# An opening group of six products, one k-tile per load, in a decoder layer kernel

## The chip, the cores and the metric

One core of a Trainium2 chip. The metric is the device time of one execution in microseconds (us); smaller is better. Engines by the names of the profile: PE = TensorE (PEld its weight loads), DVE = VectorE, ACT = ScalarE, POOL = GpSimd, SP = SyncE, which issues most loads.

## The reference

One decoder layer for 256 prompt tokens and 8 sample tokens (264 columns together), width 2048, all in float32:

```python
h = rmsnorm(x, g_pre_mix); z = h @ w_in          # one projection, split by columns into
q_m, k_m, v_m, o_m, ig, fg, q_a, k_a, v_a, gate_a, gate_b = split(z)
A = mlstm(q_m, k_m, v_m, ig, fg) * sigmoid(o_m)  # 4 heads, matrix memory
B = sliding_window_attention(rope(q_a), rope(k_a), v_a)   # 32 query heads, 4 kv heads of 64, sinks
mix = (sigmoid(gate_a) * (A @ w_branch_a) + sigmoid(gate_b) * (B @ w_branch_b)) @ w_out
x = x + rmsnorm(mix); x = x + rmsnorm(conv_ffn(rmsnorm(x)))
```

## The kernel before, in words

Everything is kept transposed: features on the 128 partitions, the 264 tokens along the row. A matrix product is made tile by tile, 128 output features at a time, over 16 k-tiles of 128. To keep float32 accuracy with the fast matmul type, each operand is split into a high and a low part, and a k-tile costs three matmuls (wh x xh, wh x xl, wl x xh; L111 to L113). `product` (L86) loads up to 8 weight tiles of 128x128 at once into `raw` (SP's queue), ScalarE casts them to `wh` (L102), VectorE subtracts to `wl` (L103), TensorE accumulates in one PSUM bank per product (`acc`, four of them). Weight buffers come in threes, so casts run at most two loads ahead of TensorE. `one` is a product of a single output tile: two loads of 8 k-tiles. `group` (L119) makes n products together, k-tile by k-tile; before, only the first six up-projections of the feed-forward part use it, with `up_chunk` (L909).

The opening: 18 warming matmuls (L155); then the four tiles of attention keys and values are made as one product of four (L192) whose k-cuts are 1, 1, 2, 2, ... tiles. For each cut `load_x` (L179) loads the inputs `xr`, scales them by the norm's weight into `xh` (ScalarE, L186) and `xl` (VectorE, L187); squares for the norm are added up in `xacc`. The norm's factor `rstd` comes from `xacc` by small matmuls (`rs`, L160), a square root, a Newton step and a transposing broadcast (`rb`, L229, L231), and is copied to `rstd` (L235). It isn't needed in the product, only behind it: the rotary tables in `katt` are multiplied by it (L245, L246). `rope` (L248) turns a tile: a shuffle and a multiplication on VectorE, a multiplication and an addition on GpSimd (`sh` L252, `qr` or `kro` L253). Turned keys are split into `KZh`, `KZl`, values are transposed (`vt`) and split into `VHL`.

Then 16 query tiles follow, four per group g of heads: `one`, `rope`, a cast of the turned tile to `Qh` on ScalarE (L449), the low part `Ql` (L450) and the sample columns `qbd` (L452) on GpSimd.

The order of work beside the products is written out by hand: `launch` queues a generator, and `step` (L68), called after each `one`-load (half a product), starts a waiting generator when the step clock allows and moves every running one on to its next `yield`. `half` (L291) is the attention of half a head group: score matmuls (`s`, L301 and L303), row maxima, exponentials, and some steps later transposes of the probabilities (`pt`) and their product with the values. The halves are launched 7 steps apart, the first right behind the fourth query product. Within this, a scheduler lays out each engine's instructions in the order in which its own model of time sees them become ready, earlier-written ones first, and those in a `high_priority` block ahead; each engine then runs its list strictly in order. `paced` adds an order between two instructions of one engine and no wait.

## Time and profile before

| | us |
|---|---|
| median of 3 runs (lowest, highest) | 1776.38 (1773.03, 1777.71) |
| profiled execution: time; span of its instructions | 1774.99; 1773.2 |
| busy: PE / PEld / DVE / ACT / POOL | 1745.8 / 1728.8 / 1222.5 / 831.0 / 259.3 |
| mean granted TensorE clock | 0.995 |

An engine's busy time is the time in which one of its instructions runs. A row of a timeline gives the start, the duration, engine, line, operation, the tile written and the tiles read, and in brackets the idle time of the engine before it and whose work ended that. Matmuls are pipelined: the start of one to the start of the next is its cost, and the durations overlap. Releasers are worked out from semaphores.

### The profile page before, as it was taken

How to read it: one execution, taken by the hardware profiler on the slowest of the kernel's cores; microseconds unless marked ns; L12 is line 12 of the kernel's file. 1: busy time of each engine (PE TensorE's matmuls, PEld its weight loads, DVE VectorE, ACT ScalarE, POOL GpSimd, SP SyncE). 2: the span in 40 equal slices, each digit the busy share in tenths (PEclk: the TensorE clock that was granted, in tenths of full speed). 3: DMA queues.
4: the chain of work that ended last, by engine and by line, in shares of the span. 5: the costliest groups of instructions: out<-in, count | busy, mean ns of one | idle time of the engine just before them, and what ended most of it. 6: DMA issues, size and time to landing. Idle time of an engine off the chain costs nothing.

```text
span 1773.2 us, 34988 instructions
## 1 busy us (share of the span) xinstructions
PE 1745.8 (98%) x14146; PEld 1728.8 (97%) x14146; DVE 1222.5 (69%) x2278; ACT 831.0 (47%) x1166; POOL 259.3 (15%) x446
## 2 busy tenths in 40 slices
PE   9999999999999999999999999999999999999996
PEld 8999999999999999999999899999999999999996
DVE  7788867546788798756644798777777777444444
ACT  6556555334555555444444554444444444434442
POOL 2542010000111121100022430000000001000002
PEclk9999999999999999999999999999999999999998
DMA  7444475555889888865555455555555555656663
GB/s 252 160 143 144 155 228 184 220 180 189 273 273 314 304 303 290 289 211 180 179 181 173 143 173 187 182 181 184 187 179 185 183 180 184 181 182 184 182 182 119
DMA packets 104090, 354.81 MB, mean 200 GB/s; under 512 B 11690, under 2 KB 16698, under 8 KB 103928
## 3 DMA queue, kind: packets, MB, share of 16 engines
q1 hardware_dynamic: 89176, 300.06, 50.9%
q0 software_dynamic: 14752, 52.52, 8.8%
q8 instruction: 110, 1.80, 0.4%
q14 instruction: 52, 0.43, 0.1%
HBM read 328.21 MB, written 24.32 MB: 199 GB/s over the span
## 4 chain that ended last, share of the span: by engine, by line
PE 83%; DVE 5%; DMA 5%; ACT 2%; issue 2%; POOL 2%; POOLq 0%; SPq 0%; ACTq 0%; DVEq 0%
PE acc L111 26%; PE acc L112 26%; PE acc L113 26%; DMA raw<-in_w_in 5%; DVE wl L103 2%; ACT wh L102 1%; PE nc L687 1%; POOL xs L867 1%; PE s L301 0%; PE nc L688 0%; PE pt L339 0%; DVE Ct L749 0%; POOL qr L253 0%; DVE cj L752 0%; PE s L303 0%
## 5 line engine op out<-in xcount | busy, mean ns | idle before, releaser
L103 DVE TENSOR_TENSOR wl<-raw,wh 128x1024 fp32r<-128x1024 f32 (+1 forms) x557 | 678.1, 1218 | 410.9 <-ACT wh L102 408.6
L102 ACT CAST wh<-raw 128x1024 fp32r<-128x1024 f32 (+1 forms) x557 | 576.6, 1036 | 785.7 <-PE acc L112 545.1
L111 PE MATMUL acc<-xh,wh 128*128 128x264 f32 x1600 | 456.6, 286 | 1.6 <-ACT wh L102 1.6
L113 PE MATMUL acc<-xh,wl 128*128 128x264 f32 x1600 | 453.9, 285 | 3.5 <-DVE wl L103 3.3
L112 PE MATMUL acc<-xl,wh 128*128 128x264 f32 x1600 | 454.2, 284 | 0.7 <-DVE xl L187 0.7
L111 PE MATMUL acc<-h2h,wh 128*128 128x264 f32 x1312 | 372.4, 284 | 0.1
L113 PE MATMUL acc<-h2h,wl 128*128 128x264 f32 x1312 | 372.4, 284 | 0.0
L112 PE MATMUL acc<-h2l,wh 128*128 128x264 f32 x1312 | 371.4, 283 | 0.0
L113 PEld LDWEIGHTS acc<-xh,wl 128*128 128x128 f32 x1600 | 300.8, 188 | 5.3 <-DVE wl L103 5.2
L111 PEld LDWEIGHTS acc<-xh,wh 128*128 128x128 f32 x1600 | 301.5, 188 | 4.2 <-ACT wh L102 2.6
L112 PEld LDWEIGHTS acc<-xl,wh 128*128 128x128 f32 x1600 | 301.1, 188 | 1.3 <-DVE xl L187 0.9
L111 PEld LDWEIGHTS acc<-h2h,wh 128*128 128x128 f32 x1312 | 246.8, 188 | 0.3 <-issue 0.3
L112 PEld LDWEIGHTS acc<-h2l,wh 128*128 128x128 f32 x1312 | 246.9, 188 | 0.0
L113 PEld LDWEIGHTS acc<-h2h,wl 128*128 128x128 f32 x1312 | 246.3, 188 | 0.0
L112 PE MATMUL acc<-yl,wh 128*128 128x264 f32 x704 | 199.9, 284 | 0.0
L113 PE MATMUL acc<-yh,wl 128*128 128x264 f32 x704 | 199.5, 283 | 0.0
L111 PE MATMUL acc<-yh,wh 128*128 128x264 f32 x704 | 199.5, 283 | 0.0
L111 PEld LDWEIGHTS acc<-yh,wh 128*128 128x128 f32 x704 | 132.5, 188 | 0.0
L113 PEld LDWEIGHTS acc<-yh,wl 128*128 128x128 f32 x704 | 132.4, 188 | 0.0
L112 PEld LDWEIGHTS acc<-yl,wh 128*128 128x128 f32 x704 | 132.3, 188 | 0.0
L852 POOL TENSOR_TENSOR nacc<-nacc,nsq 128x264 f32<-128x264 f32 x28 | 39.8, 1422 | 382.5 <-ACT nsq L845 367.6
L886 POOL COPY up_p<-E 128x2 f32<-128x2 f32 x88 | 23.6, 269 | 419.5 <-DVE E L882 414.0
(397 smaller groups left out, 2650.3 us busy)
## 6 DMA issues: line engine op xcount, KB each, us to landing
raw<-in_w_in SPq DMA_DIRECT2D x199, 512.0 KB, 4.8
raw<-in_wu SPq DMA_DIRECT2D x164, 512.0 KB, 3.7
raw<-in_wdn SPq DMA_DIRECT2D x80, 512.0 KB, 3.6
raw<-in_wb SPq DMA_DIRECT2D x32, 512.0 KB, 3.6
Ct<-in_c POOLq DMA_DIRECT2D x32, 512.0 KB, 8.4
out_c_s<-Ct POOLq DMA_DIRECT2D x32, 512.0 KB, 7.2
raw<-in_wa SPq DMA_DIRECT2D x32, 512.0 KB, 3.6
raw<-in_wo SPq DMA_DIRECT2D x32, 512.0 KB, 3.6
```

Source lines behind the costliest of these rows:

```text
L102: latest[0] = S.copy(out=wh[:, :m, :], in_=raw[:, :m, :])
L103: latest[1] = V.tensor_sub(out=wl[:, :m, :], in0=raw[:, :m, :], in1=wh[:, :m, :].bitcast(F32))
L111: T.matmul(ps[i][:, :NT], wh[:, w, :], h, start=kt == 0, stop=False)
L112: T.matmul(ps[i][:, :NT], wh[:, w, :], l, start=False, stop=False)
L113: latest[2] = T.matmul(ps[i][:, :NT], wl[:, w, :], h, start=False, stop=kt == K - 1)
L687: T.matmul(b[:, 0:n], vv[:, 0, dv], r[:, 0:n], start=x == 0, stop=False)
L852: G.tensor_add(out=acc, in0=acc, in1=sq)
L867: added = (V if k1 <= 4 else G).tensor_add(out=x2, in0=x2, in1=m)
L886: G.tensor_copy(out=up_p[:, f, :], in_=e[:, 256:258])
```

## The change

The kernel gets a new input `first`: per k-tile and partition the 264 inputs, the norm weight's 16 values of the partition and six weight tiles (four of keys and values, two of queries). `first_chunk` is the opening's new chunk function; `psk = group(6, ...)` replaces the product of four. The query tiles q0 and q1 leave the query loop, q2 is made right behind the group, ahead of the norm's small matmuls, which are put behind its first half. The values' transposes become a generator that starts three steps later. `parts` (cast, low part, sample columns of a turned query) is called one query tile later than before, and its cast is ordered behind the last weight cast of the following product; the turned tile gets a third buffer. The step clock is set so that the first `half` starts at the third step behind the query loop's first group (the seventh of the kernel, before the ninth), and the sample attention 5 steps behind the last `half` instead of 7. Host code builds `first`.

```diff
...
-            return tp.tile(list(shape), dt, tag=tag or nm, name=nm, bufs=bufs)
+            return tp.tile(list(shape), dt, tag=tag or nm, name=nm, bufs=3 if tag == "t3" else bufs)
...
-        xr = [u(nm="xr") for _ in range(4)]
...
+        pieces = [u(shape=(128, 1056), nm="piece") for _ in range(KT)]
+        with tc.high_priority(30000):
+            S.dma_start(out=pieces[0][:, 0:NT + 16], in_=a["first"][:, 0, 0:NT + 16])
+            nc.sync.dma_start(out=pieces[0][:, NT + 16:1048], in_=a["first"][:, 0, NT + 16:])
+            for k in range(1, KT):
+                nc.sync.dma_start(out=pieces[k][:, 0:1048], in_=a["first"][:, k, :])
+            nc.sync.dma_start(out=gv, in_=a["g"])
...
-        pend = []
         xacc = u(shape=(128, 2, NT), nm="xacc")
-        def flush_squares():
-            for k0, k1 in pend:
-                xc = xr[k0 // 4][:, k0 % 4:k0 % 4 + k1 - k0, :]
-                if k1 <= 2:
-                    S.activation(out=xacc[:, k0:k1, :], in_=xc, func=AF.Square)
-                else:
-                    sq = u(shape=(128, 2, NT), nm="sq")
-                    S.activation(out=sq, in_=xc, func=AF.Square)
-                    V.tensor_add(out=xacc, in0=xacc, in1=sq)
-            pend.clear()
-        def load_x(k0, k1):
-            nc.sync.dma_start(out=xr[k0 // 4][:, k0 % 4:k0 % 4 + k1 - k0, :], in_=a["x"][:, k0:k1, :])
-            if k0 == 0:
-                nc.sync.dma_start(out=gv, in_=a["g"])
-            for k in range(k0, k1):
-                xk, gk = xr[k // 4][:, k % 4, :], gv[:, 0, k:k + 1]
-                hi, lo = xh[k // 4][:, k % 4, :], xl[k // 4][:, k % 4, :]
-                S.activation(out=hi, in_=xk, func=AF.Copy, scale=gk)
-                V.scalar_tensor_tensor(out=lo, in0=xk, scalar=gk, in1=hi.bitcast(F32),
-                                       op0=ALU.mult, op1=ALU.subtract)
-            flush_squares()
-            pend.append((k0, k1))
-        psk = product(WT[T_KA:T_KA + 4], 4, xh, xl, KT, [0, 1, 2, 4, 6, 8, 10, 12, 14, 16], load_x)
-        flush_squares()
+        sqs = []
+        def first_chunk(k):
+            xk, gk = pieces[k][:, 0:NT], pieces[0][:, NT + k:NT + k + 1]
+            raw = pieces[k][:, NT + 16:1048].rearrange("p (n c) -> p n c", c=128)
+            hi, lo = xh[k // 4][:, k % 4, :], xl[k // 4][:, k % 4, :]
+            wh = wp.tile([128, 8, 128], F32R, tag="wh", name="wh")
+            wl = wp.tile([128, 8, 128], F32R, tag="wl", name="wl")
+            scaled = S.activation(out=hi, in_=xk, func=AF.Copy, scale=gk)
+            V.scalar_tensor_tensor(out=lo, in0=xk, scalar=gk, in1=hi.bitcast(F32), op0=ALU.mult, op1=ALU.subtract)
+            if k:
+                paced(scaled, latest[0])
+            latest[0] = S.copy(out=wh[:, 0:6, :], in_=raw)
+            paced(latest[0], scaled)
+            V.tensor_sub(out=wl[:, 0:6, :], in0=raw, in1=wh[:, 0:6, :].bitcast(F32))
+            if k < 2:
+                paced(S.activation(out=xacc[:, k, :], in_=xk, func=AF.Square), latest[0])
+            else:
+                if k % 2 == 0:
+                    sqs.append(u(shape=(128, 2, NT), nm="sq"))
+                paced(S.activation(out=sqs[-1][:, k % 2, :], in_=xk, func=AF.Square), latest[0])
+                if k % 2:
+                    V.tensor_add(out=xacc, in0=xacc, in1=sqs[-1])
+            return wh, wl
+        psk = group(6, xh, xl, first_chunk)
...
-        nc.sync.dma_start(out=kt_, in_=a["katt"])
+        nc.sync.dma_start(out=kt_[:, 0:C_MASK], in_=a["katt"][:, 0:C_MASK])
+        nc.sync.dma_start(out=kt_[:, C_MASK:], in_=a["katt"][:, C_MASK:])
...
-        V.tensor_copy(out=kr_[:, 0:512], in_=kt_[:, C_MGT:C_MGT + 512])
-        V.tensor_copy(out=kr_[:, 512:768], in_=kc)
...
-        rstd = rstd_from([xacc[:, 0, :], xacc[:, 1, :]], "rstd")
+        kraw, kro, qraw = u(nm="kraw"), u(nm="kro"), u(shape=(128, 2, NT), nm="qraw")
+        for f in range(4):
+            S.copy(out=kraw[:, f, :], in_=psk[f])
+        for f in range(2):
+            S.copy(out=qraw[:, f, :], in_=psk[4 + f])
+        chunk = len(marks)
+        q2 = one(WT, T_QA + 2, xh, xl)
+        for d0, d1, src in ((0, 512, kt_[:, C_MGT:C_MGT + 512]), (512, 768, kc)):
+            paced(V.tensor_copy(out=kr_[:, d0:d1], in_=src), latest[1])
+        rstd = rstd_from([xacc[:, 0, :], xacc[:, 1, :]], "rstd", after=[marks[chunk]] * 2)
...
-        kraw, kro = u(nm="kraw"), u(nm="kro")
...
-        for f in range(4):
-            S.copy(out=kraw[:, f, :], in_=psk[f])
...
-            b = bank("vt")
-            for t in range(2):
-                T.transpose(b[:, 128 * t:128 * t + 128], kro[:, 2 + f, 128 * t:128 * t + 128], ident)
-            bv = b[:, 0:256].rearrange("p (t h d) -> p t h d", t=2, h=2)
-            hi, lo = VHL[:, :, 2 * f:2 * f + 2, 0:64], VHL[:, :, 2 * f:2 * f + 2, 64:128]
-            split(hi, lo, bv)
         G.dma_start(out=o["v_new"], in_=kro[:, 2:4, 128:NT])
         V.tensor_copy(out=kvs, in_=kro[:, :, TP:NT])
+        def values():
+            for _ in range(3):
+                yield
+            for f in range(2):
+                b = bank("vt")
+                for t in range(2):
+                    T.transpose(b[:, 128 * t:128 * t + 128], kro[:, 2 + f, 128 * t:128 * t + 128], ident)
+                bv = b[:, 0:256].rearrange("p (t h d) -> p t h d", t=2, h=2)
+                hi, lo = VHL[:, :, 2 * f:2 * f + 2, 0:64], VHL[:, :, 2 * f:2 * f + 2, 64:128]
+                split(hi, lo, bv)
+        running.append(values())
...
+        turned = []
+        def parts(g, i, qr, Qh, Ql):
+            hf, jt = g % 2, g // 2
+            paced(S.copy(out=Qh[:, i, :], in_=qr[:, 0:TP]), latest[0])
+            G.tensor_sub(out=Ql[:, i, :], in0=qr[:, 0:TP], in1=Qh[:, i, :].bitcast(F32))
+            for par in range(2):
+                G.tensor_copy(out=qbd[64 * hf:64 * hf + 64, jt, :, 8 * g + 2 * i + par],
+                              in_=qr[64 * par:64 * par + 64, TP:NT])
         for g in range(4):
             Qh, Ql = u(F32R, (128, 4, 256), "Qh"), u(F32R, (128, 4, 256), "Ql")
-            hf, jt = g % 2, g // 2
             for i in range(4):
-                ps = one(WT, T_QA + 4 * g + i, xh, xl)
+                if g + i < 3 and g == 0:
+                    ps = q2 if i == 2 else qraw[:, i, :]
+                else:
+                    ps = one(WT, T_QA + 4 * g + i, xh, xl)
                 qr = tmp("qr", tag="t3")
                 rope(qr, ps)
-                S.copy(out=Qh[:, i, :], in_=qr[:, 0:TP])
-                G.tensor_sub(out=Ql[:, i, :], in0=qr[:, 0:TP], in1=Qh[:, i, :].bitcast(F32))
-                for par in range(2):
-                    G.tensor_copy(out=qbd[64 * hf:64 * hf + 64, jt, :, 8 * g + 2 * i + par],
-                                  in_=qr[64 * par:64 * par + 64, TP:NT])
+                turned.append((g, i, qr, Qh, Ql))
+                if len(turned) > 1:
+                    parts(*turned.pop(0))
+            if g == 0:
+                clock[1] = clock[0] + 3
             launch(half(g, 0, Qh, Ql), 7)
-            launch(half(g, 1, Qh, Ql), 7)
+            launch(half(g, 1, Qh, Ql), 7 if g < 3 else 5)
...
+        parts(*turned.pop())
...
+    first = A["w_in"][[64, 65, 66, 67, 48, 49]].transpose(1, 2, 0, 3).reshape(128, 16, 768)
+    gpre = i["g_pre_mix"][0].reshape(16, 128).T[:, None, :].repeat(16, 1)
+    A["first"] = np.concatenate([A["x"], gpre, first], 2)
```

## Rows read from the trace of the kernel before

**Rows 1.** Windows: stretch, length, busy (count), clock; the first two of accumulation matmuls.

```profile
0.00:7.30 7.30, 1.91 (x9) 2.09 (x10) 0.00 (x0) 0.00 (x0) 0.00 (x0) 1.00 0.62 178
7.30:31.20 23.90, 21.96 (x170) 20.84 (x168) 0.00 (x0) 0.36 (x1) 0.00 (x0) 1.00 0.88 290
...
120.00:640.00 520.00, 519.69 (x4176) 510.81 (x4176) 385.42 (x853) 267.71 (x405) 63.64 (x111) 1.00 0.66 223
```

**Rows 2.** Timeline of TensorE in the opening: start, duration, instruction.

```profile
1.26 4.33 PE L155 MATMUL warm<-warm 128*128 128x264 f32 x18 [1.26 <-DVE warm L151]
...
9.59 0.29 PE L112 MATMUL acc<-xl,wh 128*128 128x264 f32 x1
9.71 0.28 PE L113 MATMUL acc<-xh,wl 128*128 128x264 f32 x1
10.82 0.39 PE L111 MATMUL acc<-xh,wh 128*128 128x264 f32 x1 [0.82 <-ACT wh L102]
...
31.27 1.50 PE L160 MATMUL rs<-onec,xacc 128*128 128x1 f32 x12 [0.21 <-DVE xacc L176]
```

**Rows 3.** Groups by shape, 0 to 35 us: count, busy, mean ns, idle.

```profile
L186 ACT ACTIVATE xh<-xr,gv 128x264 fp32r<-128x264 f32 x16 | 7.3, 507 | 1.0 <-DMA gv<-in_g 0.9
...
L103 DVE TENSOR_TENSOR wl<-raw,wh 128x1024 fp32r<-128x1024 f32 x9 | 11.0, 1223 | 2.7 <-ACT wh L102 2.7
L187 DVE SCALAR_TENSOR_TENSOR xl<-xr,gv,xh 128x264 fp32r<-128x264 f32 x16 | 7.2, 489 | 2.4 <-ACT xh L186 2.4
L176 DVE TENSOR_TENSOR xacc<-xacc,sq 128x528 f32<-128x528 f32 x7 | 4.9, 704 | 0.1
```

**Rows 4.** Groups by shape, 980 to 1030 us, the later group of six.

```profile
L915 ACT CAST wh<-raw 128x768 fp32r<-128x768 f32 x13 | 10.7, 827 | 6.7 <-PE acc L127 4.9 <-issue 1.3 <-ACT h2h L871 0.5
...
L916 DVE TENSOR_TENSOR wl<-raw,wh 128x768 fp32r<-128x768 f32 x13 | 15.7, 1220 | 4.1 <-ACT wh L915 4.1
```

**Rows 5.** Timeline of SyncE's queue and ScalarE, first 5 us.

```profile
0.74 0.38 SPq L180 DMA_DIRECT2D xr<-in_x  x1
...
4.54 0.62 ACT L102 CAST wh<-raw 128x512 fp32r<-128x512 f32 x1 [0.61 <-DMA raw<-in_w_in]
```

**Rows 6.** DMA issues, 0 to 40 us: count, KB each, median us to landing.

```profile
raw<-in_w_in SPq DMA_DIRECT2D x13, 512.0 KB, 5.2
```

**Rows 7.** Timeline of TensorE behind the first softmax.

```profile
74.33 0.39 PE L113 MATMUL acc<-xh,wl 128*128 128x264 f32 x1 [1.08 <-DVE wl L103]
...
88.81 0.39 PE L303 MATMUL s<-KZh,Qh 128*128 128x256 f32 x1 [0.81 <-DVE PT L137]
```

**Rows 8.** Timeline of ScalarE and GpSimd, 60 to 67 us.

```profile
60.91 1.99 ACT L102 CAST wh<-raw 128x1024 fp32r<-128x1024 f32 x2
66.16 0.41 ACT L449 CAST Qh<-qr 128x256 fp32r<-128x256 f32 x1 [3.25 <-POOL qr L253]
...
64.51 1.62 POOL L253 TENSOR_TENSOR qr<-kr,sh 128x264 f32<-128x264 f32 x1
```

**Rows 9.** Waits of ScalarE, 40 to 160 us: total, times, longest.

```profile
ACT Qh L449 <- POOL qr L253: 34.1, 13, 4.3
```

**Rows 10.** Windows of the weight casts alone (line 102).

```profile
0.00:66.10 66.10, 20.00 (x20) 1.00 0.67 220
```

**Rows 11.** Timeline from the norm factor's copy to the first scores.

```profile
35.87 0.38 ACT L235 COPY rstd<-rb 128x264 f32<-128x264 f32 x1
...
52.36 0.75 POOL L253 TENSOR_TENSOR qr<-kr,sh 128x264 f32<-128x264 f32 x1 [6.74 <-DVE kr L251]
...
57.31 0.74 POOL L450 TENSOR_TENSOR Ql<-qr,Qh 128x256 fp32r<-128x256 f32 x1
...
61.97 0.40 PE L301 MATMUL s<-KZh,Qh 128*128 128x512 f32 x1
```

**Rows 12.** Windows around the later group's stops: granted clock behind the busy times.

```profile
1004.00:1007.56 3.56, 2.05 (x15) 1.64 (x14) 2.80 (x4) 3.56 (x7) 2.66 (x2) 1.00 0.22 86
1007.56:1010.97 3.41, 3.41 (x18) 3.41 (x17) 3.38 (x2) 1.15 (x2) 2.48 (x2) 0.50 0.67 186
```


## The prediction

> **What bounds the kernel now.** I read busy time by stretch first, then TensorE's timeline, then who waited for whom. TensorE sets the time: from 120 to 640 us it is busy 519.69 of 520 us [rows 1], and the change alters none of its matmuls, only their order and what they wait for. So it can give back only time in which TensorE stands still, and must be priced stall by stall in the first 120 us. Two stretches have stalls. In the opening, full-rate matmuls start 0.12 us apart (9.59, 9.71) and then one starts 1.11 us later, because it waited for its cast [rows 2]; from 7.3 to 31.2 us there are 170 accumulation matmuls in 23.9 us, so 170 x 0.122 = 20.7 are work and 3.2 are lost [rows 1]. Later, behind the first softmax, a matmul of a query product stood 1.08 us for a VectorE split, and a score matmul 0.81 us for the split of the transposed probabilities [rows 7]: 1.9 us. Between them and 120 us nothing of weight is lost. The ceiling of the change is thus 3.2 + 1.9 = 5.1 us, 0.3% of the time.
>
> **The change part by part.**
>
> *The opening in k-tiles of six.* K, V and the first two query tiles now come as 16 pieces, each one load with the inputs (264 columns) beside 768 weight columns; 17 DMAs replace 9 + 9 + the four of two query products, and all are issued ahead into 16 buffers instead of through three. Per k-tile TensorE has 18 matmuls, 18 x 0.122 = 2.2 us. ScalarE has one scaling (0.51), one cast of 768 columns (0.83) and one square, which I price like the scaling, 0.51: 1.85. VectorE has 0.49 for the low part of x, the split of 768 columns and half an add (0.70 / 2) [rows 3, 4]. The split's mean is 1.22 in the later group of six, where GpSimd adds beside it; in the old opening, with GpSimd idle, 1024 columns took 1.22 [rows 3, 4], so 768 alone come to about 0.92: VectorE 1.76 in all. With 1.22 it would be 2.06, still under 2.2. Both engines fit under TensorE, by 0.35 and 0.14 to 0.44 us a piece. Loads: 537 KB a piece in 2.2 us is 244 GB/s; the old opening moved 290 GB/s in rows of 0.5 to 2 KB [rows 1], the new rows are 4 KB. So after the first piece nothing should starve: of the 3.2 us I count 2.8 as recovered and leave 0.4 for short hitches. Bounds: 0 (each lost stretch returns elsewhere) to 3.2.
>
> *The start.* TensorE's 18 warming matmuls, begun at 1.26 and 4.33 us long with the last one's tail, keep it until 5.4 us either way [rows 2], so the first piece has until then for nothing. Before, x and the first weights (388 KB) were there for a cast at 4.54 us, 3.8 us after the first issue at 0.74 [rows 5]. The new first piece has 529 KB on two queues, in longer rows. At 4.5 and with a 0.83 us cast TensorE starts at 5.4: cost 0, which I take. If it takes as long as the median 512 KB load of this stretch, 5.2 us [rows 6], it is there at 5.9, the cast at 6.8, and TensorE starts 1.4 us late; earlier gives nothing, since the warming matmuls are in the way. Bounds: 0 to +1.4.
>
> *The end of the group.* About 178 of the 192 old matmuls were issued by 31.2 us (9 + 170 records, one counted twice) [rows 1]; without the lost 3.2 and with 288 - 178 = 110 more, the new group ends near 31.2 - 3.2 + 13.4 = 41.4 us. The next product needs an accumulator that the copy of the first key tile must free; that tile is done 15 matmuls = 1.8 us before the group's end, so the copy is hidden. If the order on TensorE finishes all six together, the copy shows, about 0.5 us. Two more copies (q0, q1) on ScalarE, the cast of constants moved behind a split, the value transposes moved to a later step, the constants' load in two parts and the norm weights behind 16 pieces on SP's queue all fall where the engine has room or the first user is many microseconds later: 0. If ScalarE's room were gone, the two copies would cost about 0.8.
>
> *The norm factor and the first scores.* This is where the change adds a possible wait. The sum of squares moves from 31.27 us to behind the first half of q2, 41.4 + 2.9 = 44.3. From it to the copied factor took 36.25 - 31.27 = 5.0 us [rows 2, 11], so the factor is there at 49.3. From the factor to the last low part that the first score step reads (q1's, ending 58.05) took 21.8 us; the scores were issued at 61.97 with 3.9 to spare [rows 11]. In the new kernel they are emitted at half-product 7 behind the group: q2, q3, q4 and half of q5 = 3.5 x 5.86 = 20.5, with the norm's own matmuls 1.8, so TensorE reaches them at 63.7, only 14.4 us after the factor. The old pace would make them ready at 49.3 + 21.8 = 71.1: a wait of 7.4. But 6.74 us of the old 21.8 GpSimd stood idle for VectorE's product of q0 [rows 11]; now q0 and q1 lie ready beside the keys. Without that idle time the pieces are ready 15.1 after the factor, 0.7 late, and the order of instructions may put other matmuls first. I take 0, nearest to the row in which the scores did not wait; bounds 0 to +7.4.
>
> The last GpSimd step in turning a query took 1.62 us for q3 and 0.75 for q0 [rows 8, 11]. The Trainium skill (SBUF — State Buffer, section Who interferes with whom) offers a reason: a VectorE instruction with two inputs in SBUF shares a read interface with GpSimd, and whoever starts first makes the other wait to its end. By that rule packing the same turns beside the same splits into 14.4 instead of 25.7 us lengthens both; this is the rival "the scores wait" below. The split of 768 columns agrees: 1.22 us beside GpSimd's adds, as long as one of 1024 columns with GpSimd idle [rows 3, 4].
>
> *Parts of turned queries behind the next product's casts.* It is meant to keep ScalarE from standing at the cast of a turned query while weight casts queue behind it; in 40 to 160 us ScalarE stood so 34.1 us in 13 waits [rows 9]. But the order asked for is there already: by 66.1 us 20 weight casts had run [rows 10], 9 of keys and values and 11 of queries, so q4's both and q5's first; the cast of q3's turned part follows at 66.16 after 3.25 us of waiting, and q5's second cast stands behind it [rows 8]. The new tie asks only that it follow q4's second. It binds nothing there, so I price it at 0 and keep both stalls [rows 7], 1.9 us. Bounds: -1.9 (both go) to +1.9 (as much again, if the later start of the attention puts two softmax steps beside a split).
>
> **Sum.** -2.8 + 0 + 0 + 0 = -2.8 us. The profiled execution took 1774.99 us (span 1773.2 and 1.8 around it), 1.4 below the median of the runs shown: 1772.2 there, 1773.6 on the median's basis, which I predict. Behind 120 us I take no difference.
>
> **The rivals.**
>
> *All stalls go.* For it: the early keys give the whole attention a calmer start, and ScalarE's 3 us waits are the root of both later stalls. Against it: the order above. -3.2 - 1.9 = -5.1, with the small hitches beside them perhaps -6: 1770.4 to 1771.3.
>
> *The scores wait.* At about 63.7 us TensorE stands at the first scores, because keys' and queries' parts are squeezed into 14.4 us; nothing can pass it on TensorE. At 4 us of wait the sum is -2.8 + 4 = +1.2. A stop of TensorE can also cost its clock: after waits in 1004 to 1007.56 us the granted clock was 0.50 of 2.4 GHz from 1007.56 to 1010.97, with 18 matmuls where 28 would fit [rows 12], 10 x 0.122 = 1.2 us lost. With 7.4 and 1.2 the sum is +5.8: 1782.2. It is slower than before from a wait of 2.8 us on, slower by over 0.3% from about 7. For it: the 71.1 above; against it: the 6.74 us of idle GpSimd.
>
> *The opening is not fed.* The first piece is 1.4 us late and the casts fall out of step as in the later group of six, so the recovered 2.8 shrinks to about 0.5: 1775.9. Against it: the load rate and the engine sums.
>
> **How the numbers follow.** Forecast 0.46 (own range 1772 to 1775.5), all stalls go 0.27, the scores wait 0.17, the opening not fed 0.10. Below 0.3% (5.3 us; about what a measurement of this kernel can tell from no change, the three runs lie 4.7 apart) is 1771.05. Faster by more: most of the second case and a little of the first, 0.27. Slower by more (over 1781.7): the far half of the third, 0.08. Within: 0.65. The range 1769 to 1778.5 holds the first, second and fourth cases and the nearer part of the third.
>
> **What would show it.** In the profile after: matmuls 0.12 apart from 5.4 to about 41.4 with no wait over 0.3 us (right) or repeated waits on casts (wrong); the factor's copy near 49 us; the first scores near 64 with no idle time before them (right) or several microseconds (third case); ScalarE's waits for turned queries still near 34 us in 13 (the order did nothing) or gone (second case). A difference made behind 120 us would make the prediction wrong in a way that none of these steps names.

## The result, and the profile after

The kernel after takes 1792.35 us (median of 6 runs, 1791.23 to 1796.8), the kernel before in the same session 1775.42 (6 runs, 1770.91 to 1779.14): ratio 1.0098, 95% interval 1.0082 to 1.0114. It is slower by 1%; predicted were 1773.6 us and no measurable difference. The profiled span is 1790.4 us (before 1773.2), the granted clock 0.990 (before 0.995).

The first view is the list of waits, here who waited for whom on TensorE, 5 to 100 us of the kernel after: total, times, longest, in us.

```profile
engine line waited for: us in total, times, longest us
PE acc L128 <- DVE wl L188: 13.5, 1, 13.5
PE s L319 <- DVE VHL L137: 5.9, 1, 5.9
```

Two stops, both far above anything in [rows 2, 7]. TensorE's timeline of the kernel after around the first and the second (start, duration, instruction, idle time with its releaser):

```profile
17.52 0.28 PE L127 MATMUL acc<-xl,wh 128*128 128x264 f32 x1
31.30 0.59 PE L128 MATMUL acc<-xh,wl 128*128 128x264 f32 x1 [13.49 <-DVE wl L188]
31.69 0.42 PE L126 MATMUL acc<-xh,wh 128*128 128x264 f32 x1
31.91 0.42 PE L127 MATMUL acc<-xl,wh 128*128 128x264 f32 x1
...
34.31 0.28 PE L126 MATMUL acc<-xh,wh 128*128 128x264 f32 x1
34.43 0.28 PE L127 MATMUL acc<-xl,wh 128*128 128x264 f32 x1
...
80.09 0.28 PE L321 MATMUL s<-KZh,Ql 128*128 128x256 f32 x1
86.23 0.79 PE L319 MATMUL s<-KZh,Qh 128*128 128x512 f32 x1 [5.86 <-DVE VHL L137]
86.82 0.63 PE L319 MATMUL s<-KZl,Qh 128*128 128x512 f32 x1
```

From 17.52 to 31.30 us no matmul starts; then they start 0.22 us apart until 34.3, where 0.12 was the pace. A wait row names only the last releaser, the split `wl` (0.95 us long). Why that split came so late stands on its own engine. VectorE's timeline of the kernel after, and the cast on ScalarE that the split reads:

```profile
12.82 0.49 DVE L183 SCALAR_TENSOR_TENSOR xl<-piece,xh 128x264 fp32r<-128x264 f32 x1
29.48 0.90 DVE L521 TENSOR_TENSOR sel<-kc 128x128 fp32r<-128x128 f32 x4 [16.16 <-DMA kc<-in_kc]
30.29 0.95 DVE L188 TENSOR_TENSOR wl<-piece,wh 128x768 fp32r<-128x768 f32 x1
```

```profile
13.08 0.83 ACT L186 CAST wh<-piece 128x768 fp32r<-128x768 f32 x1 [0.62 <-PE acc L127]
```

VectorE stood 16.16 us with four builds of `sel` (L521) at the head of its list. They read `kc`, and the sixth piece's split is behind them. `sel` is first read in the mLSTM part, at 325.6 us. The load of `kc` is the last but a few on SyncE's queue in the kernel after:

```profile
0.74 0.39 SPq L149 DMA_DIRECT2D piece<-in_first  x1
1.19 12.42 SPq L151 DMA_DIRECT2D piece<-in_first  x15
14.58 0.33 SPq L152 DMA_DIRECT2D gv<-in_g  x1
15.86 4.21 SPq L100 DMA_DIRECT2D raw<-in_w_in  x3
21.04 0.33 SPq L207 DMA_DIRECT2D kc<-in_kc  x1
```

It is issued at 21.04 us and lands 8.4 us later, at 29.4 (its row among the DMA issues: KB each, median us to landing):

```profile
kc<-in_kc SPq DMA_DIRECT2D x1, 128.0 KB, 8.4
```

That is not late beside the kernel before. There, the row on SyncE's queue, the one among the DMA issues, and the first build of `sel` on VectorE's timeline are:

```profile
26.81 0.42 SPq L201 DMA_DIRECT2D kc<-in_kc  x1
...
kc<-in_kc SPq DMA_DIRECT2D x1, 128.0 KB, 5.7
...
34.77 0.28 DVE L489 TENSOR_TENSOR sel<-kc 128x128 fp32r<-128x128 f32 x1
```

So `kc` landed at 32.5 us, and the kernel after has it 3.1 us earlier. What moved is the reader: the builds stood at 34.77 to 41.5 us in VectorE's list, behind the landing, and now come up at 13.3 us, 16 us ahead of it. By the Trainium skill (PSUM — Partial Sum Buffer, section Engine vs sequencer instructions) the lists of ScalarE, VectorE and GpSimd are strict first-in-first-out; the trace agrees, with a split whose cast ended at 13.91 us kept back until 30.29.

The clock in and behind both stops, by windows of the kernel after (the 0.50 ahead of the DMA share is the granted clock, 1.2 of 2.4 GHz; [rows 12] has one of before's such stretches):

```profile
20.61:34.26 13.65, 2.96 (x13) 2.96 (x14) 4.78 (x10) 0.00 (x0) 1.91 (x2) 0.50 0.68 263
85.46:92.29 6.83, 6.06 (x25) 5.63 (x26) 4.95 (x21) 2.03 (x5) 6.47 (x11) 0.50 0.28 94
```

A ledger ties this to the span. For each matmul I took the time to the next one's start less the first quartile of that time among matmuls of the same result tile in that trace, and added it up by stretch: what TensorE lost to waits and half clock.

| us lost, by stretch (us) | before | after | e1 | e20 | e21 |
|---|---|---|---|---|---|
| 5 to 64 | 6.1 | 17.0 | 1.3 | 2.1 | 1.7 |
| 64 to 100 | 3.8 | 9.8 | 10.6 | 7.6 | 6.3 |
| 100 to 975 | 30.5 | 28.7 | 29.7 | 28.4 | 29.4 |
| 975 to the end | 19.2 | 22.3 | 20.3 | 19.0 | 18.5 |
| all, with the first 5 us | 59.65 | 77.98 | 62.65 | 57.33 | 56.57 |

After minus before is +18.3 (the spans differ by 17.2): +10.9 up to 64 us, +6.0 up to 100, -1.8 up to 975 and +3.1 behind it. The first two hold the stops and the half clock behind them, less what the opening gained and the old stalls behind the softmax, which are not there; of the others, 1 to 3 us are within what single executions of nearly equal kernels differ by. A ledger is of one execution, which can lie several microseconds from its kernel's median.

### The profile page after: what moved, and what is told of

Read it like the earlier page. It is cut to its first block, busy times and chain, and to the rows that moved or that the text cites. A ratio compares the mean times of both kernels' runs of the same rounds, so it can differ in the third digit from the quotient of the medians.

```text
span 1790.4 us, 34996 instructions
## 1 busy us (share of the span) xinstructions
PE 1745.7 (98%) x14146; PEld 1729.9 (97%) x14146; DVE 1226.3 (68%) x2281; ACT 833.8 (47%) x1178; POOL 255.1 (14%) x446
## 4 chain that ended last, share of the span: by engine, by line
PE 85%; DMA 6%; DVE 5%; issue 2%; POOL 1%; ACT 1%; POOLq 0%; ACTq 0%; DVEq 0%
PE acc L111 26%; PE acc L112 26%; PE acc L113 26%; DMA raw<-in_w_in 3%; DVE wl L103 2%; DMA piece<-in_first 1%; PE acc L128 1%; ACT wh L102 1%; DVE Ct L781 1%; PE acc L127 1%; PE acc L126 1%; PE s L319 1%; PE nc L719 0%; DVE cj L784 0%; PE pt L357 0%
## 5 line engine op out<-in xcount | busy, mean ns | idle before, releaser
L103 DVE TENSOR_TENSOR wl<-raw,wh 128x1024 fp32r<-128x1024 f32 (+1 forms) x544 | 662.3, 1218 | 399.9 <-ACT wh L102 397.5
L102 ACT CAST wh<-raw 128x1024 fp32r<-128x1024 f32 (+1 forms) x544 | 564.2, 1038 | 783.3 <-PE acc L112 566.8
L111 PE MATMUL acc<-xh,wh 128*128 128x264 f32 x1504 | 430.1, 286 | 0.4 <-ACT wh L102 0.4
L113 PE MATMUL acc<-xh,wl 128*128 128x264 f32 x1504 | 427.6, 284 | 1.8 <-DVE wl L103 1.7
L112 PE MATMUL acc<-xl,wh 128*128 128x264 f32 x1504 | 428.1, 285 | 0.0
L113 PEld LDWEIGHTS acc<-xh,wl 128*128 128x128 f32 x1504 | 284.2, 189 | 2.6 <-DVE wl L103 2.6
L111 PEld LDWEIGHTS acc<-xh,wh 128*128 128x128 f32 x1504 | 283.9, 189 | 2.2 <-ACT wh L102 0.8
L112 PEld LDWEIGHTS acc<-xl,wh 128*128 128x128 f32 x1504 | 283.4, 188 | 0.3
```

The lines of the kernel that those rows point to most:

```text
L102: latest[0] = S.copy(out=wh[:, :m, :], in_=raw[:, :m, :])
L103: latest[1] = V.tensor_sub(out=wl[:, :m, :], in0=raw[:, :m, :], in1=wh[:, :m, :].bitcast(F32))
L111: T.matmul(ps[i][:, :NT], wh[:, w, :], h, start=kt == 0, stop=False)
L112: T.matmul(ps[i][:, :NT], wh[:, w, :], l, start=False, stop=False)
L113: latest[2] = T.matmul(ps[i][:, :NT], wl[:, w, :], h, start=False, stop=kt == K - 1)
```

## The experiments

Theories. A: the four `sel` builds, listed ahead of a split and waiting for `kc`, which lands behind their turn, are the first stop. Rival: the pieces' loads starve. For the second stop: B1, the values' transposes hold the PSUM bank of the scores; B2, the second query tile's parts are late; later, that VectorE or GpSimd has too much to do in that stretch. Ratios are against the kernel before, with 95% intervals.

**e1_sel_later.** Kernel after, `sel` behind the third query product:

```
+        held = latest[1]          # behind q2's product
...
-            V.tensor_add(out=sel[:, h, :], ...)
+            paced(V.tensor_add(out=sel[:, h, :], ...), held)
```

> The changed kernel with one tie more: the four builds of sel on VectorE, which read the constants kc, are ordered behind the low-part split of q2's second half. Theory 1 (VectorE's in-order list held: four builds that nobody needs for 400 us stand ahead of the sixth piece's split and wait for kc, whose load is queued behind all pieces): the 13.5 us stop of TensorE at 17.5 us and the half clock behind it go, some 14 to 15 us; the second stop at the first scores (5.9 us) stays, so 1776 to 1779. Rival (the pieces' loads themselves starve the opening, and sel only happens to stand there): TensorE stops in the opening for over 5 us all the same, 1785 or more.

1778.68 us, 1.0016 (1.0006 to 1.0026). The opening runs through; 14 of the 17 us are back. The norm factor is copied at 49.80 us, the first scores start at 64.16, and the second stop stays:

```profile
65.09 0.28 PE L322 MATMUL s<-KZh,Ql 128*128 128x256 f32 x1
71.23 0.80 PE L320 MATMUL s<-KZh,Qh 128*128 128x512 f32 x1 [5.86 <-DVE VHL L137]
```

**e2_kc_early.** The other end of the same wait: `sel` where it was, `kc`'s load first on the queue.

```
+            nc.sync.dma_start(out=kc, in_=a["kc"])
             nc.sync.dma_start(out=pieces[0][:, NT + 16:1048], ...)
...
-        nc.sync.dma_start(out=kc, in_=a["kc"])
```

> The changed kernel with the constants' load kc put first on SP's queue, ahead of the first piece's weights; nothing else moved, so VectorE's builds of sel still come early (by the order written, now ahead of everything else of the opening). Theory 1: if only kc's late landing held VectorE, this takes the same stop away as ordering sel later: 1776 to 1779, with at most 0.5 us lost at the start, because 128 KB more go ahead of the first weights. Rival (the order on VectorE or the pieces' loads are the fault by themselves): over 1783.

1778.52 us, 1.0017 (1.0007 to 1.0027): the same. `sel` runs at 3.4 to 4.0 us, no stop; the second stop is 6.15 us. Theory A holds from both sides.

**e12_kc_last.** Kernel after with `kc` two loads later:

```
-        nc.sync.dma_start(out=kc, in_=a["kc"])
...                                              # the two loads of katt
+        nc.sync.dma_start(out=kc, in_=a["kc"])
```

> The kernel after with kc's load issued two loads later on SyncE's queue (behind the two loads of katt, 857 KB, about 2 us by the 420 GB/s that the opening's loads reach). In VectorE's list two of the four sel builds then stand ahead of the sixth piece's weight split, one piece later than in the kernel after, and two ahead of the next. Theory: TensorE's stop begins when the pieces already split are used up, about 2 us later (19.7 in place of 17.5), and ends about 2 us later, 1.8 us behind kc's landing, near 33.3; it stays 13 to 14 us long and the time stays near 1791. Rival: the stop is the loads of the pieces themselves (the DMA queue); then its place and its end don't move.

One execution: 1792.48 us. TensorE's and VectorE's timelines of this run:

```profile
20.13 0.28 PE L127 MATMUL acc<-xl,wh 128*128 128x264 f32 x1
32.93 0.59 PE L128 MATMUL acc<-xh,wl 128*128 128x264 f32 x1 [12.52 <-DVE wl L188]
```

```profile
31.51 0.49 DVE L521 TENSOR_TENSOR sel<-kc 128x128 fp32r<-128x128 f32 x2 [15.16 <-DMA kc<-in_kc]
31.92 0.95 DVE L188 TENSOR_TENSOR wl<-piece,wh 128x768 fp32r<-128x768 f32 x1
```

The stop begins 2.6 us later, since two of the builds now stand one piece later in VectorE's list, and ends 1.6 later with the landing of `kc`. It is 12.8 us long in place of 13.8. The pieces' loads are issued almost as before (15 from 1.19 us on, in 12.99 us in place of 12.42). The rival falls.

**e4_before_parts.** Kernel before with the parts of turned queries behind the next product's casts (three buffers for `t3`, `turned`, `parts`), nothing else.

> The kernel before with the second part of the change alone: parts of turned queries made one query later, the cast tied behind the next product's weight casts, three buffers for turned tiles. The prediction says that the tie binds nothing: ScalarE's list is the same but for names, its waits for turned queries stay near 34 us in 13, and the time is within 1.5 us of before. Rival (it takes ScalarE's waits away): waits under 15 us and 1 to 2 us faster; or it is itself a part of the loss: 2 us or more slower.

1777.04 us, 1.0001 (0.9992 to 1.0010). ScalarE's waits for turned queries, 40 to 160 us, of this run:

```profile
ACT Qh L447 <- POOL qr L253: 34.0, 12, 4.3
```

Against 34.1 in 13 [rows 9]: in the old order it binds nothing.

**e6_sel_noparts.** e1 with the parts made at once (`parts(*turned.pop(0))` always, the cast not paced).

> The kernel after with the sel builds held, and the parts of the turned queries made at once as in the kernel before, not behind the next product's casts. Theory (as predicted: the reordering of the parts binds nothing): 1777 to 1780, within 0.2% of the first run's 1778.68, the wait at the first scores again about 6 us. Rival: inside the new opening the later parts are what holds the second query tile's Qh back (its cast stands behind the next weight cast); then the wait at the first scores falls below 4 us and the median to about 1775.

1775.21 us, 1.0002 (0.9993 to 1.0012). The second stop is again 6.13 us, as the theory had it; the time is not: it lies below the theory's 1777 to 1780, 0.14% under e1, without the shorter wait by which the rival would have brought it there. The two later pairs have the same sign.

**e3_sel_values.** e1 with the values' transposes after eight steps in place of three.

> As the run with sel ordered later, and the values' transposes and splits start 8 steps behind the loop's start instead of 3, so behind the first scores instead of just ahead of them. Theory 2a (the second stop comes from PSUM: the third score bank must wait for the bank of the values' transposes, whose split stands behind casts that wait for turned queries): the wait at the first scores falls from 5.9 us to under 2.5, 3 to 5 us less than the run with sel later. Theory 2b (the scores wait for q1's turned parts themselves, which come too late after the norm factor): the wait stays at 4 to 6 us and the time within 1.5 us of that run.

1779.41 us, 1.0024 (1.0014 to 1.0034). The scores stand 2.73 and 4.22 us, together no shorter than before: with the bank free they wait for the second query tile's Qh and then its Ql. B1 alone falls.

**e5_sel_scores.** e1 with the scores two steps later (`clock[1] = clock[0] + 5`).

> The kernel after with the four sel builds held behind the third query product, and the first half's scores launched two steps (two chunks of a product, some 5.9 us) later. Theory: what the first run of this study still had above the kernel before is the wait of 6.1 us at the first scores for the turned parts of the second query tile, and the half clock behind it; with the scores two steps later the parts are there, no gap over 1 us stands at the first scores, the span falls by some 6 to 8 us from 1776.4 to about 1769 to 1771, the median to about 1772 (ratio 0.998). Rival: the work only moves; the transposed probabilities or the second half's scores come late by the same two steps and the median stays at 1778 to 1779 (ratio 1.0015).

1781.33 us, 1.0031 (1.0019 to 1.0043): a miss. No wait is left at the scores, but six stops of 0.99 to 1.49 us for weights stand between 64 and 90 us; the loss from 64 to 100 is 10.6, as in e1, and later stretches lose more.

**e8_sel_qfirst.** e1 with the turns of q0 and q1 written ahead of the second key tile's turn and of the key blocks.

```
+        rope(kro[:, 0, :], kraw[:, 0, :])
+        for i in range(2):
+            rope(qrs[i], qraw[:, i, :])
+        rope(kro[:, 1, :], kraw[:, 1, :])
...
-            rope(kro[:, f, :], kraw[:, f, :])        # both key tiles, one after the other
```

> The kernel after with the sel builds held, and the turns of the first two query tiles written ahead of the second key tile's turn and of the key blocks KZh and KZl, with the scores where they were. Theory: the second query tile is late because its turn stands behind the turns of both key tiles and eight KZl subtractions in the lists of VectorE and GpSimd; moved ahead, its Qh and Ql are there by about 65 us, the wait at the first scores falls from 6.1 to at most 3 us, and the median to 1773 to 1776 (ratio 0.998 to 1.0005). Rival: the chain itself (factor, product with the tables, the two GpSimd steps, cast, difference) is as long as the distance to the scores whatever the order; the wait stays above 5 us or is taken over by KZl, and the median stays at 1778 to 1779.

1776.16 us, 1.0000 (0.9988 to 1.0012). The second tile's Ql is done at 66.2 us, but the stop is 6.23 us still. The other chain holds it: the bank of the values, whose cast stands on ScalarE behind the third tile's Qh. B2 alone falls too; in e1 the two chains end within a microsecond of each other. ScalarE's timeline of this run:

```profile
65.10 1.99 ACT L102 CAST wh<-raw 128x1024 fp32r<-128x1024 f32 x2
70.25 0.40 ACT L470 CAST Qh<-qr 128x256 fp32r<-128x256 f32 x1 [3.16 <-POOL qr L268]
70.56 0.64 ACT L136 CAST VHL<-vt 128x256 fp32r<-128x256 f32 x2
```

**e9_sel_qfirst_scores.** e8 with the scores one step later.

> The run before with the scores one step (about 3 us) later. Theory: with the parts of the second query tile early and the scores 3 us later no wait over 1 us is left there; 1771 to 1773 (ratio 0.997 to 0.999), the same as with the scores alone two steps later or a little lower. Rival: the opening's gain is given back later (half clock behind other waits), 1775 or more.

1779.35 us, 1.0023 (1.0012 to 1.0034): a miss like e5.

**e10_sel_qfirst_values, e11_best.** e8 with the values after eight steps; e11 besides with the parts at once.

> The run with the query turns ahead of the second key tile, and besides the transposes of the values five steps later. Theory: the first scores are held by two chains that end within a microsecond of each other, the second query tile's Ql (72.0 us in the first run of this study) and the bank that the values' transposes hold until their cast, which ScalarE makes behind the third tile's Qh (70.6 us); either one alone was taken away and the other kept the wait at 6 to 7 us. With both away the wait is what Ql leaves, from 64.9 to 66.2 us: under 2 us in place of 6.2, no half clock at 69 to 76 us, and the median 1771 to 1774 (ratio 0.998 to 0.9995). Rival: VectorE and ScalarE, in the order in which their lists stand, are late with the next weights by the same time (the runs with the scores later showed waits of 1 to 2 us for wl there), so that three or four such waits take the place of the one: 1776 or more.

> The same with the parts of the turned queries made at once, as in the kernel before. Theory: the order of the parts binds nothing, so this is within 0.15% of the run beside it, 1771 to 1775. Rival: the parts behind the next casts cost the 1 to 2 us by which the two runs with and without them differed, and this one is the faster by that.

1778.63 us, 1.0017 (1.0007 to 1.0027), and 1776.84, 1.0008 (0.9996 to 1.0020). Both chains are away and the wait at the scores is under 1 us, as expected. The time did not follow: four and five stops of 1.2 to 1.8 us, for weights, took its place, with a stretch of half clock; 11.0 and 10.7 us are lost from 64 to 100. The rival is what happened.

**e13_kz_later, e14_kz_later_noparts.** e10 and e11 with the second key tile's blocks twelve steps later.

> The run with the query turns ahead and the values later, and besides the blocks KZh and KZl of the second key tile (eight casts and copies on ScalarE and VectorE, which only the third pair of heads needs) made twelve steps later. Theory: what TensorE loses between 64 and 100 us (10 to 11 us in every order tried, 3.8 in the kernel before) is the time that VectorE, ScalarE and GpSimd need for all that hangs on the norm factor, while TensorE has fewer products left to run beside it; four of the eight KZl subtractions (some 0.5 us each) and four KZh casts out of that stretch take 2 to 4 us of the loss, and the median falls to 1773.5 to 1776 (ratio 0.999 to 1.0003). Rival: the loss hangs on the longest chain (factor, turn, cast, difference) and not on the amount of work: it stays at 10 to 11 us and the median at 1777 to 1779.

> The same with the parts of the turned queries made at once. Theory: within 0.1% of the run beside it. Rival: it is lower by 0.1% or more, as the two other pairs of runs with and without the later parts were (0.14% and 0.09%), and then the later parts cost about 2 us in the new opening, which the pair in the kernel before doesn't show.

1779.61 us, 1.0022 (1.0009 to 1.0035), and 1774.28, 0.9996 (0.9984 to 1.0009). The loss from 64 to 100 us stays at 11.0 and 11.1, as the rival had it. But e14 lies 0.26% below e13, more than its own theory allowed, and as low as e20 below, where that loss is 7.6. So the loss in this stretch of one execution and the median time do not go together.

**e16_no_kzl_values.** e10 without the eight KZl subtractions; the keys' low part stays zero, so this part of the computation is left out.

> The run with the query turns ahead and the values later, with all eight KZl subtractions left out (the keys' low parts stay zero; the products with them are still made). Theory of the amount of work: VectorE is 4 to 5 us less busy between 54 and 69 us, GpSimd's neighbours run at their shorter times, and TensorE's loss between 64 and 100 us falls by 4 to 6 us; median 1772 to 1775. Rival: it stays at 10 to 11 us, the median at 1777 to 1779.

1777.91 us, 1.0016 (1.0003 to 1.0029): no gain. Windows of e10 and of this run (TensorE, its loads, VectorE, ScalarE, GpSimd):

```profile
54.00:74.00 20.00, 18.77 (x145) 17.60 (x144) 17.56 (x33) 7.95 (x15) 15.97 (x23) 1.00 0.39 128
54.00:74.00 20.00, 17.60 (x135) 16.57 (x134) 11.33 (x23) 8.23 (x17) 18.80 (x30) 1.00 0.35 105
```

VectorE is busy 11.33 of 20 us (17.56 in e10) and the loss is still 10.2. VectorE's amount alone is not the bound. GpSimd is busy 18.80 us here and 15.97 in e10, with about the same loss, so its busy time alone does not tell the loss either.

**e17_turns_on_vector, e19_turns_wholly.** e14 with the GpSimd product of the first four turns on VectorE; e19 with product and sum.

```
-            G.tensor_mul(out=sh, in0=sh, in1=sinT)
-            G.tensor_add(out=dst, in0=kr, in1=sh)
+            (V if turns[0] <= 4 else G).tensor_mul(...)
+            (V if turns[0] <= 4 else G).tensor_add(...)     # e19 only
```

> The run with the second key tile's blocks later and the parts at once, and besides the first product of the first four turns (shuffled tile by the sine table) made by VectorE in place of GpSimd. Theory: GpSimd's amount of work is what TensorE waits for between 64 and 100 us; in that run GpSimd is busy 4.6 to 4.7 us of each 5 from 54 to 74 us, ScalarE's weight casts stand behind casts Qh that wait 2 to 3 us for GpSimd's qr, and the weights' low parts behind these. Four products (0.85 to 0.9 us each) out of GpSimd's list against four of 0.42 us more on VectorE take 2 to 4 us of the 11 that are lost; median 1771.5 to 1773.5. Rival: VectorE is the bound; the loss stays at 11 or grows, 1774 or more.

> The same with both GpSimd steps of the first four turns (product and sum) on VectorE: eight instructions, some 7 to 9 us, leave GpSimd's list, and 3.4 us come to VectorE's. Theory of GpSimd's amount: the loss of TensorE between 64 and 100 us falls from 11 to 4 to 7 us, GpSimd's busy share from 54 to 74 us falls below 0.75, and the median to 1769 to 1772 (ratio 0.9965 to 0.998), below the kernel before. Rival: VectorE becomes the bound, the loss stays at 9 to 11 us and the median at 1774 to 1778.

1774.03 us, 0.9991 (0.9980 to 1.0002), and 1774.39, 0.9990 (0.9981 to 0.9999). In e17 the loss falls from 11.1 to 8.0 us, as expected, but the time lies above the expected 1773.5. In e19 it falls only to 9.5; the theory had 4 to 7 and a time of at most 1772, and the rival's figures are what came. Neither time is measurably below e14's, 0.9996 (0.9984 to 1.0009).

**e20_sel_turns_wholly.** The first four turns wholly on VectorE, in e1, whose order is that of the kernel after.

> The kernel after with the sel builds held, its order otherwise as it was, and the first four turns wholly on VectorE. There VectorE is busy 14.6 of 15 us from 54 to 69 us and GpSimd 11.5. Theory of GpSimd's amount: the wait of 6.1 us at the first scores falls to 2 to 4 us, the median to 1774 to 1776. Rival, VectorE's amount: the wait grows by 1 to 3 us, 1779 or more.

1774.25 us, 0.9996 (0.9988 to 1.0005), 0.2% below e1. The wait at the first scores falls from 6.14 to 1.93 us. The groups by shape of VectorE, 54 to 69 us (count, busy, mean ns), of e1 and of e20:

```profile
L103 DVE TENSOR_TENSOR wl<-raw,wh 128x1024 fp32r<-128x1024 f32 x4 | 5.9, 1467 | 0.0
L284 DVE TENSOR_TENSOR KZl<-kro,KZh 64x256 fp32r<-64x256 f32 x8 | 5.0, 631 | 0.1
```

```profile
L103 DVE TENSOR_TENSOR wl<-raw,wh 128x1024 fp32r<-128x1024 f32 x5 | 6.6, 1327 | 0.0
L287 DVE TENSOR_TENSOR KZl<-kro,KZh 64x256 fp32r<-64x256 f32 x8 | 3.3, 418 | 0.1
```

And the windows of the same two:

```profile
54.00:69.00 15.00, 11.37 (x92) 11.03 (x90) 14.65 (x26) 6.90 (x13) 11.53 (x16) 1.00 0.41 126
```

```profile
54.00:69.00 15.00, 13.78 (x113) 13.49 (x111) 14.87 (x34) 8.33 (x15) 6.77 (x8) 1.00 0.54 167
```

VectorE makes 34 instructions in place of 26 in the same 15 us, because each is shorter: the same eight subtractions take 418 ns with GpSimd less busy (6.77 us in place of 11.53) and 631 with GpSimd at its turns. One by one they tell it more plainly. In e1 (VectorE's timeline, and GpSimd's beside it) the second of the eight ran beside a product of GpSimd, the third beside nothing:

```profile
57.44 1.13 DVE L284 TENSOR_TENSOR KZl<-kro,KZh 64x256 fp32r<-64x256 f32 x1
58.58 0.42 DVE L284 TENSOR_TENSOR KZl<-kro,KZh 64x256 fp32r<-64x256 f32 x1
...
57.26 1.02 POOL L267 TENSOR_TENSOR sh<-sh,katt 128x264 f32<-128x264 f32 x1
```

Over all traces of this case, the 78 such subtractions with no two-input instruction of GpSimd beside them took 406 to 424 ns, the 74 with one 397 to 1589, 777 on average. So what GpSimd had to do cost twice, on GpSimd and on VectorE. This agrees with the rule of the Trainium skill (SBUF — State Buffer, section Who interferes with whom) that the prediction gave to its third case.

**e21_turns_waits.** e20 with the two waits left there moved: the values after eight steps, the first half's probability transposes one step later.

```
-            for _ in range(3):          # values()
+            for _ in range(8):
-            yield  (x4)                 # half(), ahead of the transposes
+            for _ in range(5 if g == 0 and q4 == 0 else 4):
+                yield
```

> The last run (sel builds held, the first four turns wholly on VectorE, order otherwise as in the kernel after), and besides the two waits that were left in it after the first scores moved: the values' transposes five steps later (the 1.9 us wait for their bank) and the transposes of the first half's probabilities one step later (waits of 2.0 and 1.2 us for P). Theory: TensorE's loss between 64 and 100 us falls from 7.6 to 4 to 5.5 us, near the 3.8 of the kernel before, and the opening's 4 to 5 us show in the time: median 1770 to 1772.5 (ratio 0.997 to 0.9985). Rival: VectorE, which has 4.4 of each 5 us to do there, hands the waits on to the next weights' low parts; the loss stays at 7 to 9 us and the median at 1774 to 1776.

1772.05 us, 0.9978 (0.9967 to 0.9989): 0.22% below the kernel before; of the other runs only e19's interval also stays below 1. The loss from 64 to 100 us is 6.3, above the 4 to 5.5 expected; 2.3 of it are waits for P, which VectorE makes:

```profile
PE pt L359 <- DVE P L350: 2.3, 2, 1.3
```

With the parts at once it was not run.

## Why the prediction was wrong

- *What bounds the kernel*: right. TensorE's stalls in the first 100 us decide (+16.9 of the ledger's +18.3), and nothing behind them needs a new mechanism.
- *The opening in k-tiles of six*: right once theory A's stop is away. In e1 the loss from 5 to 31 us falls from 4.7 to 1.0, so 3.7 come back where 2.8 were counted; the first matmul starts 0.3 to 0.7 us later (*The start*, taken as 0).
- *The end of the group*: **the step that failed.** It put at 0 what stands on SyncE's queue beside and behind the 16 pieces, since all of it falls "where the engine has room or the first user is many microseconds later". `kc` is one of these loads, though the list does not name it. The step looked for the user that needs the result, not for the first instruction in an engine's list that reads the load, and it took VectorE's list to keep its order. In its place the runs showed four idle builds of `sel` that had moved from 34.77 us to the turn at 13.3 us, ahead of a landing at 29.4: they stopped VectorE for 16.16 us and TensorE for 13.8, and the clock fell. That only this wait is at fault is shown from both sides (e1, e2). That the list was laid out by a model of time in which `kc` is there early fits e12, where a later `kc` put two builds one piece later; why that model moved the builds ahead is not shown.
- *The norm factor and the first scores*: times right (factor 49.80 against 49.3, scores 64.16 against 63.7 in e1), size wrong. The wait was taken as 0 between bounds of 0 and 7.4; it is 6.1, and the parts are there at 72.0 us, by the old pace 71.1. The argument against it was 6.74 us of idle GpSimd [rows 11]. VectorE's timeline of the kernel before shows what that idle time waited for:

```profile
43.87 0.45 DVE L250 STREAM_SHUFFLE sh<-acc 128x264 f32<-128x264 f32 x1
...
51.79 0.43 DVE L251 TENSOR_TENSOR kr<-acc,katt 128x264 f32<-128x264 f32 x1
```

q0 was there at 43.87 us already; its product stood behind the splits of keys, values and weights in VectorE's list, and these stay. In e1 the idle time falls to 3.03 us (1.75, 0.84 and 0.44, all for VectorE). The 3.7 us gained are spent again: from 67.59 to 71.27 us GpSimd makes steps of the third and fourth query tile, which its list has ahead of the second tile's Ql, though the Qh that this reads was there at 67.45 (timelines of ScalarE and GpSimd in e1):

```profile
67.05 0.40 ACT L466 CAST Qh<-qr 128x256 fp32r<-128x256 f32 x1 [3.08 <-POOL qr L268]
...
68.41 1.60 POOL L268 TENSOR_TENSOR qr<-kr,sh 128x264 f32<-128x264 f32 x1
...
71.27 0.73 POOL L467 TENSOR_TENSOR Ql<-qr,Qh 128x256 fp32r<-128x256 f32 x1
```

The values' transposes in a later step, also put at 0 (under *The end of the group*), hold the scores' bank as long (e3, e8). "The scores wait" (0.17) was the right rival for this part, half clock included; the lengthening that it named is there (e20), but the longer steps of the queries on GpSimd (1.59 and 1.62 us against 0.75) are made up by shorter ones of the keys (1.77 against 3.60).
- *Parts of turned queries*: right at 0 in the old order (e4; in the kernel after ScalarE still waits 32.3 us in 12). In the new order the three pairs e1/e6, e10/e11, e13/e14 are 0.14, 0.09 and 0.26% slower with it; their ledgers differ between 100 and 299 us (10.5 against 9.2, 10.2 against 9.5, 14.1 against 10.1; the 14.1 is from e13's slowest execution, 7.0 us above its median). That it costs some there is likely, not settled.
- *Sum*: -2.8 + 0 should have been, in the ledger, +10.9 up to 64 us (about -3.7 for the opening, 13.7 for the stop and 1.4 for the slow matmuls behind it) and +6.0 from there to 100 (the stop of 6.1 and the slow matmuls behind it, less the old late stalls [rows 7], which the prediction kept and which are not there up to 100 us).

What stays open: what sets the 64-to-100 loss, and how far it sets the time. Taking work from GpSimd moved the loss (10.6 to 7.6, 11.1 to 8.0 and 9.5); taking it from VectorE alone or reordering did not (10.1 to 11.1 in twelve runs). How much of that is GpSimd's amount and how much the order of the lists is not settled, and medians do not follow the loss of one execution: with 10.4 and 11.1 us lost e6 and e14 are at 1.0002 and 0.9996, with 10.6 e1 at 1.0016. That the opening's 4 to 5 us are given back there because the same turns and splits have fewer products beside them fits the times (14.4 us from the factor to the scores in e1, 26.1 in the kernel before), but no run shows it by itself.

## What to carry to other kernels

When loads or lists are laid out anew, list for every load each instruction that reads it on every engine, the ones that nobody needs soon above all, and look at its turn and at what stands behind it in the list: the price is the landing time less that turn, not the need of the result. The load need not have become later; here it landed 3.1 us earlier, and its readers came up some 21 us earlier. When a wait row names an engine that is itself idle, follow that engine's own wait before naming a cause. When TensorE's work moves ahead of a stretch, add up the other engines' work in that stretch over what is left; if removing one wait only makes another, count the loss over the whole stretch.

## What was not expected of the hardware

The granted clock fell after stops far shorter than the first. In e10, behind a stop of 1.79 us (from 74.98) and within the next of 1.49 (to 78.48), it was 0.50 from 78.03 on; the window from there, of this run:

```profile
78.03:81.45 3.42, 2.97 (x13) 2.97 (x14) 3.35 (x21) 2.35 (x5) 2.34 (x5) 0.50 0.45 152
```

And the same stop did not always bring it. The 1.81 us ahead of the first product of the later group stand in all 20 traces; half clock followed 0.2 to 1.4 us behind them in seven, as in the kernel before from 980.25 us, and not in thirteen, as in e1, where the clock stayed 1.00. One profile thus carries a microsecond or two of chance per such stretch [rows 12], about as much as most edits here moved; only the timed ratios tell them apart.
